# Hybrid decoder layer on one Trainium2 core: the conv gate, the h * c product and the taps stay in the products' PSUM banks

## The chip, the cores and the metric

The kernel runs on one NeuronCore of a Trainium2 chip, as one launch. The metric is the device time in microseconds (us) of that core. TensorE (PE) has the matmuls, VectorE (DVE), ScalarE (ACT) and GpSimd (POOL) the elementwise work, SyncE (SP) issues the transfers. DVE and ACT read and write SBUF and the eight PSUM banks into which PE writes; POOL's operations in this kernel touch SBUF alone.

## The reference, cut to what matters

1024 tokens of width 1024 in float32. The part around the change is the mixer:

```
z = rms_norm(x, norm1_g) @ w_in
cb, cc, ch = split(z[..., :1536], 3)          # B, C, h of the conv group, 512 columns each
rq, rk, rv, rg = split(z[..., 1536:], 4)      # retention: 4 heads of 128 columns each
y_conv = cb * causal_dwconv3(cc * ch, conv_w) # up[t] * w0 + up[t + 1] * w1 + up[t + 2] * w2
y_conv = group_rms_norm(y_conv, conv_norm_g, 8)
o = chunkwise_retention(rotary(q), rotary(k) / sqrt(128), v)
y_ret = group_rms_norm(o, ret_norm_g, 4) * silu(rg)
x = x + concat(y_conv, y_ret) @ w_out
x = x + relu(rms_norm(x) @ w_up) ** 2 @ w_down
out = rms_norm(x)
```

## The kernel before, in words

Tiles are 128 x 1024: 128 columns of a product on the partitions, the 1024 tokens along the free dimension, in two halves of 512 (one PSUM bank each). A float32 matmul is done as three in fp32r: the high and the low part (names `uh`, `ul`, `wh`, `wl`) as high*high, low*high and high*low. The low part of each weight tile is a subtraction, `wl<-r,wh`, on DVE or POOL, behind an ACT cast `wh<-r`.

The first norm's factor per token is R (square root of the mean square, inverted); R2 is R squared and shares its name `ssq` in the rows. It isn't applied to the input but to the projection's result: to B and the gates by R, to C * h by R2.

The columns of `w_in` are 24 tiles f. Tiles 0 to 11 are the conv group in triples i = 0 to 3: C is f = 3i, h is f = 3i + 1, B is f = 3i + 2. Tiles 12 to 19 are q and k, 20 to 23 the gates. The order is the list `IN_TURNS` (line 40): first q and k, then tiles 0, 1, 2, 3, 20 as *whole* tiles (two halves in two banks), then the pairs (4,5), (6,7), (8,9), (10,11), then 21 whole, and 22 and 23 at the end (line 925). A pair is done by one step of a Strassen-Winograd scheme: seven products of half size, `product(n)`, and DVE additions that put them together into the quadrants c11, c12 (first tile of the pair) and acc, c22 (second tile). Its inputs t1 to t4 are made by `rights(j)`: subtractions `xs<-xs` and splits `U<-xs` (ACT cast, then `U<-xs,U` on POOL or DVE).

What happens to a finished half is in `conv_h` (line 677), `conv_b` (702) and `gate` (721), picked by `use` (736) and called from `whole` (744), `pair_in` (824) and the loop at 925. Before the change:

- C: two ACT copies into SBUF (whole tiles), or DVE additions that end in SBUF (pairs).
- h: `a = C * h`, `a *= R2` (POOL or DVE), `cv = a * w2` on ACT, then two DVE taps `cv += a shifted by 1 or 2 * w`.
- B: `o = B * R`, `o *= cv`, then the group norm: a PE product with `blkr` for the mean of squares, and two DVE operations on `o`.
- gates: `g = z * R`, SiLU on ACT, times the retention's output.

A planner decides at build time. Each of these is a Python generator that yields the engines that it could run on (`yield (pool, dve)`) or what it waits for; `background` (428) gives it the engine whose modelled clock is earliest, and writes it into that engine's instruction stream. So a changed operation also moves others. PE's order is fixed by the lists; two pools, `pm` and `pr`, hold four banks each and are taken in turn. A bank can be written again only when its last reader is done.

The retention runs beside tiles 0, 1 and the first `rights`. Its steps are one chain through four engines: PE scores (L625, `b<-v,h`), DVE `h<-b,bk,causal` and `S<-S,b`, ACT `h<-b,bz`, the small DVE and ACT operations on `m` (128x2, the group norm of the step), ACT `h<-b,m`, and PE transposes (L663, `b<-ident,h`).

Of the kernel before, what the change touches and what calls it, by code (L numbers as in the profile page):

```python
# [10 lines left out]
F32 = mybir.dt.float32  # L11
F32R = mybir.dt.float32r
AF = mybir.ActivationFunctionType
ALU = mybir.AluOpType
PSUM = bass.MemoryType.PSUM

P = 128
D = 1024
T = 1024
H = 512  # L20
# [21 lines left out]
SLOT, LOOK, PE_MARGIN, LATE = 2.72, 3.2, 1.2, 0.0  # L42
# [37 lines left out]
def hybrid_layer(  # L80
# [18 lines left out]
    now, clock, procs, got = [0.0], {}, [], {}  # L99
    act = Engine(nc.scalar, 0.13, 0.95, now, clock)  # L100
    pool = Engine(nc.gpsimd, 0.2, 2.5, now, clock)
    dve = Engine(nc.vector, 0.13, 1.04, now, clock, pool)
# [11 lines left out]
    xp = mixer.enter_context(tc.tile_pool(name="xp", bufs=1))  # L114
# [5 lines left out]
    def nm(s):  # L120
        n_[0] += 1
        return f"{s}{n_[0]}"

    def unit(dt=F32, s="u"):
        return big.tile([P, T], dt, tag="u", name=nm(s))
# [6 lines left out]
    def bank(pool_=None):  # L132
        return (pool_ or pm).tile([P, H], F32, tag="b", name=nm("b"))
# [4 lines left out]
    hs = [slice(0, H), slice(H, T)]  # L138
# [90 lines left out]
    for turn in IN_TURNS + IN_END:  # L229
        if isinstance(turn, tuple):  # L230
            o = Left(mix, 1)
# [11 lines left out]
    b = bank(pr)  # L243
# [14 lines left out]
    less_g = cp.tile([P, 4], F32, name="less_g")  # L258
# [26 lines left out]
    R = xp.tile([P, T], F32, name="R")  # L285
# [136 lines left out]
    def spawn(gen, ready=None, late=0.0):  # L422
        Task(gen, now[0] if ready is None else ready, late).go()

    def mark(key, eng):
        got[key] = clock[eng]
# [33 lines left out]
    def slot():  # L460
        now[0] += SLOT
# [58 lines left out]
    def tile_in(evac):  # L520

        out = [bank() for _ in hs]
        for quarter in range(4):
            c, at = quarter // 2, quarter % 2
            if at == 0:
                piece = parts.pop(0)
            mm(
                piece, out,
                lambda n, k: (uh[4 * c + k][:, hs[n]], ul[4 * c + k][:, hs[n]]),
                quarter == 0, quarter == 3, range(2 * at, 2 * at + 2),  # L530
            )
            slot()
            if at:
                prepare()
            if quarter == 1 and once:
                once.pop()()
            if quarter == 3:
                evac(out)
            tick()
# [132 lines left out]
                mark(("retention", p), act)  # L672


    a_of, cvs = {}, {}

    def conv_h(i, half, z, psum):

        a, sl = a_of[i], hs[half]
        eng = dve if psum else (yield (pool, dve))  # L680
        eng.tensor_mul(a[:, sl], a[:, sl], z)
        eng = yield (pool, dve)
        eng.tensor_mul(a[:, sl], a[:, sl], R2[:, sl])
        mark(("a", i, half), eng)
        if half:
            yield "a", i, 0
        yield (act,)
        if i not in cvs:
            cvs[i] = unit(s="cv")
        cv = cvs[i]  # L690
        w = [sm[:, CW + 3 * i + j : CW + 3 * i + j + 1] for j in range(3)]
        act.activation(cv[:, sl], a[:, sl], AF.Copy, scale=w[2])
        yield (dve,)
        for j in (1, 2):
            to = slice(max(sl.start, j), sl.stop)
            dve.scalar_tensor_tensor(
                cv[:, to], a[:, to.start - j : to.stop - j], w[2 - j], cv[:, to],
                ALU.mult, ALU.add,
            )
        mark(("cv", i, half), dve)  # L700

    def conv_b(i, half, z, out, psum):
        sl = hs[half]
        o = out[:, sl]
        eng = dve if psum else (yield (pool, dve))
        eng.tensor_mul(o, z, R[:, sl])
        yield "cv", i, half
        eng = yield (pool, dve)
        eng.tensor_mul(o, o, cvs[i][:, sl])
        y[i] = out  # L710

        def done(rt, less):
            yield (dve,)
            dve.scalar_tensor_tensor(o, o, less_g[:, i : i + 1], rt, ALU.mult, ALU.mult)
            yield (dve,)
            dve.scalar_tensor_tensor(o, less, 1.5, o, ALU.subtract, ALU.mult)
            mark(("y", i, half), dve)

        asked.append((o, blkr, 1.0 / 64, done, clock[eng], LATE * half))

    def gate(h, half, z, g, psum):
        sl = hs[half]
        eng = dve if psum else (yield (pool, dve))
        eng.tensor_mul(g[:, sl], z, R[:, sl])
        yield (act,)
        act.activation(g[:, sl], g[:, sl], AF.Silu)
        yield "o", h, half
        yield (dve,)
        o = o_n[h, half]
        dve.scalar_tensor_tensor(  # L730
            o[:, sl], g[:, sl], sm[:, RG + h : RG + h + 1], o[:, sl], ALU.mult, ALU.mult
        )
        y[4 + h] = o
        mark(("y", 4 + h, half), dve)

    def use(f, half, out, z, psum):

        if f >= 20:
            return gate(f - 20, half, z, out, psum)
        if f % 3 == 1:  # L740
            return conv_h(f // 3, half, z, psum)
        return conv_b(f // 3, half, z, out, psum)

    def whole(f):
        def evac(z):
            if f < 20 and f % 3 == 0:
                out = a_of[f // 3] = unit(s="a")
                for half, sl in enumerate(hs):
                    act.copy(out[:, sl], z[half])
                return  # L750
            out = None if f < 20 and f % 3 == 1 else unit(s="z")
            for half in range(2):
                spawn(use(f, half, out, z[half], True), clock[dve])

        tile_in(evac)

# [61 lines left out]
    for j in range(4):  # L818
        for c, name in ((0, "11"), (1, "21"), (2, "22")):
            k = j + (4 if c else 0)  # L820
            sl = hs[c == 2]
            U.setdefault(name, [None] * 4)[j] = (uh[k][:, sl], ul[k][:, sl])

    def pair_in(fs):
        out = [unit(s="z") for _ in range(2)]
        (c11, c12), (acc, c22) = ([o[:, sl] for sl in hs] for o in out)
        for at, n in enumerate(UP_ORDER):
            if not got.get("pairs") and n in (5, 6, 7, 4):
                for j in range(4):
                    force(({5: "t1", 6: "t2", 7: "t3", 4: "t4"}[n], j))  # L830
            b = product(n, (pm, pr)[at % 2])
            slot()
            prepare()
            ready = None
            if n == 1:
                act.copy(acc, b)
            if n == 2:
                dve.tensor_add(c11, acc, b)
                ready = 0, 0
            if n == 5:  # L840
                b5 = b
            if n in (6, 7, 4):
                dve.tensor_add(acc, acc, b)
            if n == 6:
                dve.tensor_add(c12, acc, b5)
            if n == 7:
                dve.tensor_add(c22, acc, b5)
                ready = 1, 1
            if n == 3:
                dve.tensor_add(c12, c12, b)  # L850
                ready = 0, 1
            if n == 4:
                ready = 1, 0
            if ready:
                f, half, o = fs[ready[0]], ready[1], out[ready[0]]
                if f < 20 and f % 3 == 0:
                    a_of[f // 3] = o
                else:
                    spawn(use(f, half, o, o[:, hs[half]], False), clock[dve], LATE * half)
            tick()  # L860
        got["pairs"] = now[0]

# [48 lines left out]
    for half in range(2):  # L911
        for f, (z, banks, pieces) in ends.items():
            for c in range(2):
                if half == 0:
                    pieces.append(parts.pop(0))
                mm(
                    pieces[c], [banks[half]],
                    lambda n, k: (uh[4 * c + k][:, hs[half]], ul[4 * c + k][:, hs[half]]),
                    c == 0, c == 1,
                )  # L920
                slot()
                if half:
                    prepare()
                if c:
                    spawn(use(f, half, z, banks[half], True), clock[dve])
                tick()
    for half in range(2):
        while any(("split" if half == 0 else "y", idx, half) not in got for idx in range(KT)):
# [322 lines left out]
    for at, (n, p) in enumerate((n, p) for n in MLP_ORDER for p in range(EARLY)):  # L1251
        b = early[p].product(n)
# [106 lines left out]
    def finish(wide, sl, out):  # L1359
        n = sl.stop - sl.start  # L1360
        r = spread(wide)
        if n == H:
            act.copy(R3, r)
            r = R3

        def scale(g):
            o3 = out[g][:, : 2 * n].rearrange("p (a b) -> p a b", b=n)
            dve.tensor_mul(o3, o3, r[:, None, :].to_broadcast([P, 2, n]))
            dst = outT[2 * g * P : 2 * (g + 1) * P, sl].rearrange("(a p) b -> p a b", p=P)
            nc.sync.dma_start(dst, o3)  # L1370

        finishing.extend(lambda g=g: scale(g) for g in range(KT // 2))
# [27 lines left out]
    for sl in (slice(0, H), slice(H, TE)):  # L1400
        n = sl.stop - sl.start
        out = []
# [56 lines left out]
    o = unit(s="end")  # L1459
# [104 lines left out]
```

## Time and profile before

| | us |
|---|---|
| median of three runs | 1071.01 (1069.68 to 1071.92) |
| the profiled execution | 1070.03 |
| its span, first to last instruction | 1068.1 |
| PE busy | 1054.8 (99%) |
| DVE busy | 870.8 (82%) |
| POOL busy | 561.6 (53%) |
| ACT busy | 463.6 (43%) |

The span lies 1.9 us under the profiled execution's own time, and that execution 1.0 us under the median. The granted TensorE clock is full throughout (0.999 on average). PE is busy in 99% of the span, so the table alone says only that time is lost or won where PE waits; the engines' shares do not say where. In a row of the timeline the first number is the start, the second the duration, and `[0.66 <-ACT h L74]` is the idle time of the engine before it and what ended it. Line 74 is the helper that records every elementwise operation, so tiles and operations tell them apart, not lines.

### The profile page before, as it was taken

Reading aid. Unit: us, or ns where it says so; the run is one execution under the profiler, and the core shown is the slowest. Engines: PE = TensorE matmul, PEld = TensorE weight load, DVE = VectorE, ACT = ScalarE, POOL = GpSimd, SP = SyncE. Lnnn points to the kernel's source line nnn. Section 1 sums busy time; section 2 is a strip of 40 time slices with the busy share of each in tenths; the row PEclk is TensorE's granted clock in tenths of the full one; section 3 lists DMA queues with packets and bytes.
Section 4 is the critical chain, followed back from the end, with each engine's and each line's share of the span. In section 5 each row is a group of like instructions: output and inputs, shape, how many; then the busy total and the mean of one; then the engine's idle time right before and its main releaser. Section 6 shows DMA issues by size and latency. Waiting matters only on the chain.

```text
span 1068.1 us, 13853 instructions
## 1 busy us (share of the span) xinstructions
PE 1054.8 (99%) x4860; PEld 879.2 (82%) x4860; DVE 870.8 (82%) x1231; ACT 463.6 (43%) x906; POOL 561.6 (53%) x381
## 2 busy tenths in 40 slices
PE   9999999999999999999999999999999999999997
PEld 8888888788888888788788888888888888888886
DVE  7446546799998665799999989999899899899955
ACT  8211445673437444443343433343443434334453
POOL 6334324367854233559458267277186295384552
PEclk9999999999999999999999999999999999999999
DMA  7121122122223733051221211211301201200204
GB/s 276 65 58 42 38 80 70 63 95 80 69 69 129 256 115 123 11 187 39 61 59 49 79 31 50 90 30 50 99 21 50 89 21 49 90 21 19 69 30 158
DMA packets 39685, 82.25 MB, mean 77 GB/s; under 512 B 4544, under 2 KB 5696, under 8 KB 39616
## 3 DMA queue, kind: packets, MB, share of 16 engines
q1 hardware_dynamic: 39328, 80.85, 23.5%
q8 instruction: 38, 0.62, 0.2%
q10 hardware_dynamic: 288, 0.52, 0.1%
q14 instruction: 31, 0.25, 0.1%
HBM read 71.92 MB, written 9.44 MB: 76 GB/s over the span
## 4 chain that ended last, share of the span: by engine, by line
PE 90%; DVE 6%; ACT 2%; issue 1%; POOL 1%; DVEq 0%; ACTq 0%; POOLq 0%
PE b L403 55%; PE b L1277 23%; PE b L357 4%; PE b L1386 4%; DVE t L74 1%; DVE wl L74 1%; DVE x L74 1%; DVE m L74 1%; ACT h L74 1%; DVE q L74 1%; DVE V L74 1%; PE b L339 0%; PE b L595 0%; PE b L1436 0%; PE b L246 0%
## 5 line engine op out<-in xcount | busy, mean ns | idle before, releaser
L74 ACT CAST wh<-r 128x512 fp32r<-128x512 f32 x286 | 176.6, 620 | 326.4 <-PE b L403 134.4
L403 PE MATMUL b<-U,wh 128*128 128x512 f32 x1024 | 315.8, 390 | 2.0 <-DVE x L74 1.2
L74 DVE TENSOR_TENSOR wl<-r,wh 128x512 fp32r<-128x512 f32 x250 | 232.8, 933 | 89.0 <-ACT wh L74 87.8
L74 POOL TENSOR_TENSOR r<-r,r 128x512 f32<-128x512 f32 x136 | 210.2, 1548 | 114.1 <-DVE wl L74 66.1
L1277 PE MATMUL b<-V,wh 128*128 128x512 f32 x784 | 242.0, 389 | 0.7 <-POOL V L74 0.4
L403 PEld LDWEIGHTS b<-U,wh 128*128 128x128 f32 x1024 | 191.7, 188 | 43.2 <-issue 2.4
L74 DVE TENSOR_TENSOR x<-x,b 128x512 f32<-128x512 f32 (+1 forms) x312 | 195.5, 673 | 28.8 <-PE b L1386 14.3
L403 PE MATMUL b<-U,wl 128*128 128x512 f32 x512 | 199.2, 389 | 0.0
L1277 PEld LDWEIGHTS b<-V,wh 128*128 128x128 f32 x784 | 147.1, 188 | 32.4 <-POOL V L74 0.9
L74 POOL TENSOR_TENSOR t<-t,t 128x512 f32<-128x512 f32 x70 | 106.3, 1523 | 96.4 <-ACT t L74 50.4
L1277 PE MATMUL b<-V,wl 128*128 128x512 f32 x392 | 152.5, 389 | 0.0
L74 POOL TENSOR_TENSOR wl<-r,wh 128x512 fp32r<-128x512 f32 x36 | 51.4, 1432 | 119.3 <-ACT wh L74 116.5
L403 PEld LDWEIGHTS b<-U,wl 128*128 128x128 f32 x512 | 96.1, 188 | 19.9
L403 PE MATMUL b<-uh,wh 128*128 128x512 f32 x304 | 102.3, 396 | 0.0
L403 PE MATMUL b<-ul,wh 128*128 128x512 f32 x304 | 100.5, 390 | 0.0
L403 PE MATMUL b<-uh,wl 128*128 128x512 f32 x304 | 100.2, 389 | 0.0
L1277 PEld LDWEIGHTS b<-V,wl 128*128 128x128 f32 x392 | 73.6, 188 | 15.2
L74 POOL TENSOR_TENSOR V<-t,V 128x512 fp32r<-128x512 f32 x35 | 49.6, 1418 | 67.0 <-ACT V L74 67.0
L74 DVE TENSOR_TENSOR t<-t,b 128x512 f32<-128x512 f32 x112 | 75.8, 677 | 1.7 <-POOL t L74 1.2
L74 ACT ACTIVATE t<-t 128x512 f32<-128x512 f32 x64 | 40.2, 631 | 81.2 <-DVE t L74 80.5
L74 DVE TENSOR_TENSOR V<-t,V 128x512 fp32r<-128x512 f32 x63 | 70.3, 1116 | 0.0
L403 PEld LDWEIGHTS b<-uh,wl 128*128 128x128 f32 x304 | 57.0, 188 | 12.3
(177 smaller groups left out, 1431.3 us busy)
## 6 DMA issues: line engine op xcount, KB each, us to landing
r<-w_up_t SPq DMA_DIRECT2D x64, 256.0 KB, 2.6
r<-w_down_t SPq DMA_DIRECT2D x56, 256.0 KB, 2.7
r<-w_in_t SPq DMA_DIRECT2D x48, 256.0 KB, 2.7
xt<-xT SPq DMA_DIRECT2D x16, 256.0 KB, 5.4
xs<-xT SPq DMA_DIRECT2D x8, 512.0 KB, 5.0
r<-w_out_t SPq DMA_DIRECT2D x16, 256.0 KB, 2.7
x<-xT SPq DMA_DIRECT2D x8, 512.0 KB, 7.9
k<-x SPq DMA_DIRECT2D x6, 512.0 KB, 3.0
```

The costliest lines, as they stand in the source:

```text
L74: return f(out, *args, **kw)
L357: nc.tensor.matmul(vb[i], a[k][:, i * P : (i + 1) * P], b[k // 2][:, vs], start=(k == 0 and a is uh and b is vh), stop=(k == KT - 1 and a ...
L403: nc.tensor.matmul(b, a[:, k, :], rhs(n, k)[r], start=(start and i == 0), stop=(stop and i == len(ops) - 1),)
L1277: nc.tensor.matmul(b, a, r, start=(i == 0), stop=(i == len(ops) - 1))
L1386: nc.tensor.matmul(z, a, b, start=(k == 0 and t == 0), stop=(k == 3 and t == 2))
```

## The change

C is multiplied by R2 as soon as it is in SBUF (`conv_c`), in place of `a * R2` after the product with h. `h * C` is written back into h's bank, ACT and both taps read it there; the last two columns of the first half are copied to a small tile, `edge`, from which the second half's first columns are made with two small taps. In a pair the last addition of a quadrant goes into the bank of a product (`to`) in place of SBUF, and gate and B are multiplied from the bank by R on DVE, never on POOL. The norm's two operations on `o` become one on `less` in its bank (all `b<-b,r`) and one on `o`.

```diff
-    def conv_h(i, half, z, psum):
+    def conv_c(i, half):
+        eng = yield (pool, dve)
         a, sl = a_of[i], hs[half]
-        eng = dve if psum else (yield (pool, dve))
-        eng.tensor_mul(a[:, sl], a[:, sl], z)
-        eng = yield (pool, dve)
         eng.tensor_mul(a[:, sl], a[:, sl], R2[:, sl])
-        mark(("a", i, half), eng)
+        mark(("c", i, half), eng)
+
+    def conv_h(i, half, z):
+        sl = hs[half]
+        yield "c", i, half
+        yield (dve,)
+        dve.tensor_mul(z, z, a_of[i][:, sl])
         if half:
             yield "a", i, 0
         yield (act,)
...
-        act.activation(cv[:, sl], a[:, sl], AF.Copy, scale=w[2])
+        act.activation(cv[:, sl], z, AF.Copy, scale=w[2])
+        if not half:
+            edges[i] = xp.tile([P, 2], F32, tag="edge", name=nm("edge"), bufs=4)
+            act.copy(edges[i], z[:, H - 2 :])
+            mark(("a", i, 0), act)
         yield (dve,)
         for j in (1, 2):
-            to = slice(max(sl.start, j), sl.stop)
+            to = slice(sl.start + j, sl.stop)
             dve.scalar_tensor_tensor(
-                cv[:, to], a[:, to.start - j : to.stop - j], w[2 - j], cv[:, to],
-                ALU.mult, ALU.add,
+                cv[:, to], z[:, : H - j], w[2 - j], cv[:, to], ALU.mult, ALU.add
             )
+            if half:
+                to = slice(sl.start, sl.start + j)
+                dve.scalar_tensor_tensor(
+                    cv[:, to], edges[i][:, 2 - j :], w[2 - j], cv[:, to], ALU.mult, ALU.add
+                )
...
-    def conv_b(i, half, z, out, psum):
+    def conv_b(i, half, z, out):
...
-        eng = dve if psum else (yield (pool, dve))
-        eng.tensor_mul(o, z, R[:, sl])
+        dve.tensor_mul(o, z, R[:, sl])
...
             yield (dve,)
-            dve.scalar_tensor_tensor(o, o, less_g[:, i : i + 1], rt, ALU.mult, ALU.mult)
+            dve.scalar_tensor_tensor(less, less, 1.5, rt, ALU.subtract, ALU.mult)
             yield (dve,)
-            dve.scalar_tensor_tensor(o, less, 1.5, o, ALU.subtract, ALU.mult)
+            dve.scalar_tensor_tensor(o, less, less_g[:, i : i + 1], o, ALU.mult, ALU.mult)
...
-        eng = dve if psum else (yield (pool, dve))
-        eng.tensor_mul(g[:, sl], z, R[:, sl])
+        dve.tensor_mul(g[:, sl], z, R[:, sl])
...
     def whole(f):
...
+                    spawn(use(f, half, out, None), clock[act], 4.0)
...
     def pair_in(fs):
...
+        def finish(i, half, c, a, b, to):
+            f = fs[i]
+            if kind(f) == "c":
+                to = c
+                a_of[f // 3] = out[i]
+            dve.tensor_add(to, a, b)
+            spawn(use(f, half, out[i], to), clock[dve], LATE * half)
...
             if n == 2:
-                dve.tensor_add(c11, acc, b)
-                ready = 0, 0
+                finish(0, 0, c11, acc, b, b)
...
             if n == 7:
-                dve.tensor_add(c22, acc, b5)
-                ready = 1, 1
+                finish(1, 1, c22, acc, b5, b5)
             if n == 3:
-                dve.tensor_add(c12, c12, b)
-                ready = 0, 1
+                finish(0, 1, c12, c12, b, b)
             if n == 4:
-                ready = 1, 0
+                finish(1, 0, acc, acc, b, b)
```

On POOL, between tiles 0 and 2. Before; `a_1532` is C * h of the first triple, `xs_1465`, `xs_1686` and `xs_1687` belong to `rights`, `U_1569` and `U_1912` are its splits:

```order
L74 TENSOR_TENSOR xs_1465<-xs_1465 128x512
L74 TENSOR_TENSOR U_1569<-xs_1465,U_1569 128x512
L74 TENSOR_TENSOR wl_1642<-r_1412,wh_1641 128x512
L74 TENSOR_TENSOR wl_1756<-r_1480,wh_1755 128x512
L74 TENSOR_TENSOR a_1532<-a_1532,ssq 128x512
L74 TENSOR_TENSOR xs_1686<-xs_1686 128x512
L74 TENSOR_TENSOR wl_1875<-r_1526,wh_1874 128x512
L74 TENSOR_TENSOR xs_1687<-xs_1687 128x512
L74 TENSOR_TENSOR U_1912<-xs_1686,U_1912 128x512
```

After; here `z_1532` is C of the first triple, and `xs_1688` what `xs_1686` was:

```order
L74 TENSOR_TENSOR xs_1465<-xs_1465 128x512
L74 TENSOR_TENSOR z_1532<-z_1532,ssq 128x512
L74 TENSOR_TENSOR U_1569<-xs_1465,U_1569 128x512
L74 TENSOR_TENSOR wl_1644<-r_1412,wh_1643 128x512
L74 TENSOR_TENSOR wl_1758<-r_1480,wh_1757 128x512
L74 TENSOR_TENSOR xs_1688<-xs_1688 128x512
L74 TENSOR_TENSOR wl_1877<-r_1526,wh_1876 128x512
L74 TENSOR_TENSOR xs_1689<-xs_1689 128x512
L74 TENSOR_TENSOR wl_1981<-r_1641,wh_1980 128x512
```

The multiplication by R2 stands right behind `xs_1465` and ahead of `U_1569`, three POOL operations earlier, and the split `U_1912` has left POOL.

On DVE at the same place of the program, one retention step, after:

```order
L74 SCALAR_TENSOR_TENSOR m_1554<-m_1554,bq 128x2
L74 TENSOR_TENSOR m_1558<-m_1558 128x2
L74 SCALAR_TENSOR_TENSOR m_1558<-m_1558,m_1554 128x2
L74 SCALAR_TENSOR_TENSOR m_1558<-m_1558 128x2
L74 TENSOR_TENSOR U_1566<-xs_1464,U_1566 128x512
L74 TENSOR_TENSOR z_1532<-z_1532,ssq 128x512
L74 SCALAR_TENSOR_TENSOR h_1592<-b_1587,bk,causal 128x128 x2
L74 SCALAR_TENSOR_TENSOR S_1605<-S_1551,b_1598 128x128 x2
```

Before, the row `z_1532<-z_1532,ssq` isn't there, and the scores' `h` follows `U_1566` directly: the second half of the multiplication by R2 has come in front of the retention's `h` and `S`.

On DVE at the end of the last pair, after; `b_2828` is the bank of the product n = 3, `z_2546` is C, `cv_2772` the convolution, `edge_2774` the two columns:

```order
L74 TENSOR_TENSOR z_2728<-z_2728,b_2807 128x512
L74 TENSOR_TENSOR z_2727<-z_2728,b_2778 128x512
L74 TENSOR_TENSOR wl_2844<-r_2746,wh_2843 128x512
L74 TENSOR_TENSOR b_2828<-z_2727,b_2828 128x512
L74 TENSOR_TENSOR b_2828<-b_2828,z_2546 128x512
L74 SCALAR_TENSOR_TENSOR cv_2772<-b_2828,sm,cv_2772 128x511
L74 SCALAR_TENSOR_TENSOR cv_2772<-edge_2774,sm,cv_2772 128x1
L74 SCALAR_TENSOR_TENSOR cv_2772<-b_2828,sm,cv_2772 128x510
L74 SCALAR_TENSOR_TENSOR cv_2772<-edge_2774,sm,cv_2772 128x2
```

Before, the bank of this product (there `b_2803`) was read once, by the addition:

```order
L74 TENSOR_TENSOR z_2702<-z_2702,b_2782 128x512
L74 TENSOR_TENSOR z_2701<-z_2702,b_2758 128x512
L74 TENSOR_TENSOR z_2701<-z_2701,b_2803 128x512
L74 TENSOR_TENSOR z_2536<-z_2536,z_2701 128x512
```

Now five operations use it, with one of ACT between the product with C and the first tap. The second half of tile 21 is the next to write that bank.

## Rows read from the trace of the kernel before

**Rows 1.** PE waits by line: releaser, total us, count, longest

```profile
PE b L663 <- ACT h L74: 2.3, 5, 0.7
```

**Rows 2.** Windows, us: busy time and count of PE, PEld, DVE, ACT, POOL; clock

```profile
213.00:345.00 132.00, 132.00 (x584) 109.28 (x584) 120.22 (x133) 71.91 (x115) 90.01 (x60) 1.00 0.27 87
```

**Rows 3.** PE timeline, retention: start, duration, instruction, idle before

```profile
179.86 0.39 PE L625 MATMUL b<-v,h 128*128 128x128 f32 x2
181.20 0.38 PE L663 MATMUL b<-ident,h 128*128 128x128 f32 x2
...
197.00 0.44 PE L663 MATMUL b<-ident,h 128*128 128x128 f32 x2 [0.66 <-ACT h L74]
...
206.61 0.59 PE L663 MATMUL b<-ident,h 128*128 128x128 f32 x2 [0.73 <-ACT h L74]
...
210.32 0.58 PE L663 MATMUL b<-ident,h 128*128 128x128 f32 x2 [0.35 <-ACT h L74]
```

**Rows 4.** POOL timeline, 172 to 208 us

```profile
172.28 1.29 POOL L74 TENSOR_TENSOR xs<-xs 128x512 f32<-128x512 f32 x1 [0.63 <-DVE xs L74]
176.75 1.30 POOL L74 TENSOR_TENSOR U<-xs,U 128x512 fp32r<-128x512 f32 x1 [3.17 <-ACT U L74]
...
193.57 1.27 POOL L74 TENSOR_TENSOR a<-a,ssq 128x512 f32<-128x512 f32 x1
194.81 1.26 POOL L74 TENSOR_TENSOR xs<-xs 128x512 f32<-128x512 f32 x1
...
207.73 1.30 POOL L74 TENSOR_TENSOR U<-xs,U 128x512 fp32r<-128x512 f32 x1 [1.99 <-ACT U L74]
```

**Rows 5.** DVE timeline, the same stretch

```profile
174.00 0.16 DVE L74 SCALAR_TENSOR_TENSOR m<-m,bq 128x2 f32<-128x2 f32 x1 [0.94 <-ACT h L74]
...
176.18 0.69 DVE L74 TENSOR_TENSOR U<-xs,U 128x512 fp32r<-128x512 f32 x1 [1.20 <-ACT U L74]
176.79 0.60 DVE L74 SCALAR_TENSOR_TENSOR h<-b,bk,causal 128x128 f32<-128x128 f32 x2
...
193.90 0.97 DVE L74 TENSOR_TENSOR m<-m 128x2 f32<-128x2 f32 x1 [0.27 <-ACT m L74]
...
194.90 1.19 DVE L74 SCALAR_TENSOR_TENSOR m<-m,m 128x2 f32<-128x2 f32 x1
...
208.21 0.83 DVE L74 SCALAR_TENSOR_TENSOR m<-m,bq 128x2 f32<-128x2 f32 x1 [0.61 <-ACT h L74]
```

**Rows 6.** POOL timeline, 222 to 225 us

```profile
222.94 1.39 POOL L74 TENSOR_TENSOR wl<-r,wh 128x512 fp32r<-128x512 f32 x1 [2.84 <-ACT wh L74]
```

**Rows 7.** DVE timeline, 222 to 225 us

```profile
222.50 0.69 DVE L74 TENSOR_TENSOR U<-xs,U 128x512 fp32r<-128x512 f32 x1
...
223.10 1.79 DVE L74 TENSOR_TENSOR U<-xs,U 128x512 fp32r<-128x512 f32 x1
```

**Rows 8.** ACT timeline of the step at 175 us

```profile
175.53 1.14 ACT L74 CAST U<-xs 128x512 fp32r<-128x512 f32 x2
177.49 0.62 ACT L74 ACTIVATE h<-b,bz 128x128 f32<-128x128 f32 x2 [0.82 <-DVE h L74]
...
179.68 0.62 ACT L74 ACTIVATE h<-b,m 128x128 f32<-128x128 f32 x2 [0.62 <-DVE m L74]
```

**Rows 9.** Groups by operation, 160 to 345 us: busy, mean ns | idle before

```profile
L74 DVE TENSOR_TENSOR z<-z,b 128x512 f32<-128x512 f32 x28 | 19.0, 679 | 0.4
L74 DVE SCALAR_TENSOR_TENSOR cv<-z,sm,cv 128x512 f32<-128x512 f32 x4 | 5.8, 1461 | 0.1
L74 ACT ACTIVATE cv<-z,sm 128x512 f32<-128x512 f32 x4 | 2.9, 725 | 11.1 <-POOL z L74 11.1
```

**Rows 10.** PE timeline at the end of the last pair

```profile
305.76 0.39 PE L484 MATMUL b<-s,blkr 128*128 128x512 f32 x1
...
311.43 0.62 PE L403 MATMUL b<-uh,wh 128*128 128x512 f32 x2
```

**Rows 11.** DVE timeline there

```profile
309.07 2.19 DVE L74 TENSOR_TENSOR z<-z,b 128x512 f32<-128x512 f32 x3
```

More of the change, by code (lines that the diff above doesn't have):

```diff
@@ L672, in retention @@
                 mark(("retention", p), act)
-    a_of, cvs = {}, {}
-    def conv_h(i, half, z, psum):
+    a_of, cvs, edges = {}, {}, {}
+    def conv_c(i, half):
+        eng = yield (pool, dve)
         a, sl = a_of[i], hs[half]
-        eng = dve if psum else (yield (pool, dve))
-        eng.tensor_mul(a[:, sl], a[:, sl], z)
-        eng = yield (pool, dve)
         eng.tensor_mul(a[:, sl], a[:, sl], R2[:, sl])
-        mark(("a", i, half), eng)
+        mark(("c", i, half), eng)
[4 more added lines that the diff above has]
+        dve.tensor_mul(z, z, a_of[i][:, sl])
         if half:
@@ L713, in done, with gate @@
             yield (dve,)
-            dve.scalar_tensor_tensor(o, o, less_g[:, i : i + 1], rt, ALU.mult, ALU.mult)
+            dve.scalar_tensor_tensor(less, less, 1.5, rt, ALU.subtract, ALU.mult)
             yield (dve,)
-            dve.scalar_tensor_tensor(o, less, 1.5, o, ALU.subtract, ALU.mult)
+            dve.scalar_tensor_tensor(o, less, less_g[:, i : i + 1], o, ALU.mult, ALU.mult)
             mark(("y", i, half), dve)
         asked.append((o, blkr, 1.0 / 64, done, clock[eng], LATE * half))
-    def gate(h, half, z, g, psum):
+    def gate(h, half, z, g):
         sl = hs[half]
-        eng = dve if psum else (yield (pool, dve))
-        eng.tensor_mul(g[:, sl], z, R[:, sl])
+        dve.tensor_mul(g[:, sl], z, R[:, sl])
         yield (act,)
@@ L734, in gate, with kind, use @@
         mark(("y", 4 + h, half), dve)
[L736 to L742, printed above, removed]
+    def kind(f):
+        return "g" if f >= 20 else "chb"[f % 3]
+    def use(f, half, out, z):
+        if kind(f) == "g":
+            return gate(f - 20, half, z, out)
+        if kind(f) == "c":
+            return conv_c(f // 3, half)
+        if kind(f) == "h":
+            return conv_h(f // 3, half, z)
+        return conv_b(f // 3, half, z, out)
     def whole(f):
         def evac(z):
-            if f < 20 and f % 3 == 0:
-                out = a_of[f // 3] = unit(s="a")
+            out = None if kind(f) == "h" else unit(s="z")
+            if kind(f) == "c":
+                a_of[f // 3] = out
                 for half, sl in enumerate(hs):
                     act.copy(out[:, sl], z[half])
+                    spawn(use(f, half, out, None), clock[act], 4.0)
                 return
-            out = None if f < 20 and f % 3 == 1 else unit(s="z")
             for half in range(2):
-                spawn(use(f, half, out, z[half], True), clock[dve])
+                spawn(use(f, half, out, z[half]), clock[dve])
         tile_in(evac)
@@ L826, in pair_in @@
         (c11, c12), (acc, c22) = ([o[:, sl] for sl in hs] for o in out)
+        def finish(i, half, c, a, b, to):
+            f = fs[i]
+            if kind(f) == "c":
+                to = c
+                a_of[f // 3] = out[i]
+            dve.tensor_add(to, a, b)
+            spawn(use(f, half, out[i], to), clock[dve], LATE * half)
         for at, n in enumerate(UP_ORDER):
@@ L833, in pair_in @@
             prepare()
-            ready = None
             if n == 1:
@@ L837, in pair_in @@
             if n == 2:
-                dve.tensor_add(c11, acc, b)
-                ready = 0, 0
+                finish(0, 0, c11, acc, b, b)
             if n == 5:
                 b5 = b
-            if n in (6, 7, 4):
+            if n in (6, 7):
                 dve.tensor_add(acc, acc, b)
@@ L846, in pair_in @@
             if n == 7:
-                dve.tensor_add(c22, acc, b5)
-                ready = 1, 1
+                finish(1, 1, c22, acc, b5, b5)
             if n == 3:
-                dve.tensor_add(c12, c12, b)
-                ready = 0, 1
+                finish(0, 1, c12, c12, b, b)
             if n == 4:
-                ready = 1, 0
[L854 to L859, printed above, removed]
+                finish(1, 0, acc, acc, b, b)
             tick()
@@ L924, in hybrid_layer @@
                 if c:
-                    spawn(use(f, half, z, banks[half], True), clock[dve])
+                    spawn(use(f, half, z, banks[half]), clock[dve])
                 tick()
```

## The prediction, made before the changed kernel ran

> **What bounds the kernel now.** I read the table of engine shares first: PE is busy in 99% of the span, so an edit on DVE, POOL or ACT counts only where PE waits for them. The list of PE's waits says where that is. The part that the change touches, from the first tiles to the end of the projection, has one entry of weight: L663, the retention's transposes, which wait for ACT's `h`, 2.3 us in five waits [rows 1]. Next, the windows: from 213 to 345 us, where all four pairs, tiles 2, 3, 20 and 21 are evacuated, PE is busy for 132.00 of 132.00 us, while DVE is busy for 120.22 and POOL for 90.01 [rows 2]. A shorter DVE buys nothing there. It can only lose: if a bank is held so long that PE finds it taken.
>
> The retention's steps come third. Three of the five waits lie in the stretch that changes, at 197.00, 206.61 and 210.32 (0.66, 0.73 and 0.35 us) [rows 3]. Their origin is on the engine behind ACT. DVE's `m` operations on two columns take 0.16 us where nothing is beside them, but the one at 193.90 took 0.97 and ended with POOL's `a<-a,ssq`, the one at 194.90 took 1.19 and ended with POOL's `xs<-xs`, and the one at 208.21 took 0.83 and ended with POOL's split U [rows 4, 5]. So an SBUF operation of DVE that starts beside one of POOL ends with it. Where DVE has the next one queued, POOL still goes first: `wl` starts at 222.94, when DVE's U from 222.50 is nearly done; the next U of DVE starts at 223.10 and takes 1.79, to 0.56 us behind the end of `wl` at 224.33 [rows 6, 7]. An operation that reads a bank isn't held: the scores' `h` from 176.79 (two of 128x128, with a factor and a mask in SBUF) takes 0.60 us beside POOL's U from 176.75 [rows 4, 5], and 28 additions of a bank average 679 ns, where taps in SBUF average 1461 [rows 9].
>
> [...]
>
> **The change, part by part.**
>
> *Bank operations in place of SBUF ones.* Taps, products and the norm's factor move into banks, at about 0.68 us in place of up to 1.46 [rows 9]. In 213 to 345 us this is worth 0 on the path, since PE never waits [rows 2]; the cover is the queue of matmuls. [...]
>
> *The multiplication of C by R2 moves into a retention step.* This is the term that costs. (a) Before, POOL's `xs` ends at 172.28 + 1.29 = 173.57. Now the multiplication of the first half follows at once, for 1.27 us as `a<-a,ssq` took, until 174.83. DVE's `m` at 174.00 would start in it and end with it: 174.83 in place of 174.16, +0.67 on the chain. (b) ACT's two casts U [rows 8] start that much later, DVE's U runs to 177.53 in place of 176.87. POOL's U, whose cast is ready, then takes its turn and ends 1.14 us later (as 224.33 follows DVE's 223.19), at 178.67; the queued second half of the multiplication ends 0.56 us behind it, at 179.23. (c) Only then comes the scores' `h`, at 179.15 (it began 0.08 before its forerunner's end) in place of 176.79: the chain is +2.36. Behind it on DVE stand `S` and the step's `m`, and ACT's `h` and then PE wait for those. (d) PE: the score product at 179.86 writes a bank that ACT's `h<-b,bz` has to have read; that ends at 177.49 + 0.62 + 2.36 = 180.47, so PE waits 0.6 there. L663 at 181.20 needs ACT's `h<-b,m`, which ends at 179.68 + 0.62 + 2.36 = 182.66, or 1.46 late; together +1.5 us.
>
> From below: if DVE's second multiplication went ahead of POOL's U it would take 0.69, the chain would be +1.35 at `h`, and L663's operand would be ready at 181.65, 0.45 late. If nothing collided, 0. From above: both collisions in full, 2 x 1.3 + 0.69 = 3.3 on the chain, +2.4 for PE after the 0.9 that it has in hand (181.20 less 180.30). I take 1.5, since 222 to 225 us show this very order.
>
> *One collision less at 197.* `a<-a,ssq` is gone from 193.57. At most the 0.97 us become 0.16. But `xs` stands right behind it in POOL's stream, its input was ready, and so it moves up into the same place. From both sides 0 and 0.81; I take 0.2, near the lower end, and the shift falls from +1.5 to +1.3. The wait at 206.61 hangs on work that the change leaves there: 0.
>
> *One split less on POOL at 207.73.* U moves to DVE, ahead of the `m` operations. The `m` at 208.21 falls from 0.83 to 0.16, a gain of 0.67 on the chain, of which PE can use its wait of 0.35 and the slower transposes behind it (0.58 in place of 0.38 or 0.44), 0.55. Shift +0.75. From both sides 0 (U on DVE itself delays `m`) and 0.67.
>
> *Banks of tile 1 held by the taps.* Before, one multiplication freed each bank; now ACT's scaling and two taps, the last ones behind the retention's `m` operations. Tile 2 writes these banks next, just behind 210.32. At 0.68 us a tap the last one ends about when PE arrives: I take +0.2, between 0 and 2 x 0.78 = 1.56 (each tap at 1461 ns). Shift +0.95.
>
> *The bank of product n = 3 of the last pair.* Before, it was free with the last of three additions, 309.07 + 2.19 = 311.26; tile 21's second half needs it at 311.66 (the second of two matmuls from 311.43) [rows 10, 11], 0.4 us in hand, and the additions stood behind two taps of 3.2 us. Now: the product ends behind the two norm matmuls at 306.15, then the addition into the bank, the multiplication by C and one `wl` ahead of them (3 x 0.68), ACT's scaling 0.73 [rows 9], two hand-overs of 0.25, a tap 0.68, an edge tap of at most 0.2 (as a small operation alone), the second tap 0.68: 310.98. In hand 0.68, cost 0.
>
> *The rest.* The edge copy and six edge taps are small operations, some 0.2 us each and at worst 1.19 [rows 5]; in 213 to 345 us they lie beside full PE. The norm's DVE operations stay two, one of them in a bank: 0. SP's transfers and PE's list are the same but for a few places of the norm's products.
>
> Sum: +1.5 - 0.2 - 0.55 + 0.2 = +0.95. The profiled execution takes 1070.03 and would take 1070.98; it lies 0.98 under the median of its runs, 1071.01, so the forecast in the median's terms is 1071.96, told as 1071.9. About 0.2%, 2.1 us, is what a measurement of this kernel can tell from no change.
>
> **The rivals.**
>
> *B, little is lost.* The second multiplication goes ahead of POOL's split, or the retention makes good what it lost before 197. Then 0.45 - 0.2 - 0.55 + 0.2 = -0.1: 1070.9. For it: the later waits take up delay. Against: rows 6 and 7.
>
> *B2, the collisions all vanish.* If operations on banks leave the retention's DVE work free, the 2.3 us of rows 1 are the most that can go: 1068.7. Against: two of the five waits lie ahead of the change, and 206.61 isn't touched.
>
> *C, slower: a bank is held.* If an operation in a bank, reading and writing it or with SBUF operands beside POOL, takes as long as the tap in SBUF, 1.46, the last pair's chain has four of them: 4 x 0.78 = 3.1, less 0.68 in hand, 2.45 us that PE waits at 311.66; at tile 2's banks up to 1.56. With 0.95: +5.0, 1076. It decides from 0.68 + 0.68/4 = 0.85 us for each such operation. For it: rows 9 have no tap from a bank with an SBUF accumulator. Against: `h<-b,bk,causal` has such operands and wasn't held.
>
> That the change does not do what it says: the order shows that it does, so this gets no chance of its own.
>
> **How the numbers follow.** Forecast 0.64 (its own range 1070.9 to 1073.0), B 0.14, B2 0.05, C 0.17. The range leaves out the lower part of B2 and the upper half of C: 1069.7 to 1074.2. Faster by over 0.2% is under 1068.9, most of B2 and a little of B: 0.07. Slower by over 0.2% is over 1073.15: C and the upper tail of the forecast, 0.19. Within it: 0.74.
>
> **What would show it.** Right: DVE's `m` near 174.0 lasts about 0.8 us; `z<-z,ssq` on DVE near 177 takes 1.7; L663 waits near 181 for the first time; taps from a bank take about 0.68; PE stays full from tile 2 to 345. Wrong: no wait at 181 (B); PE waits at a whole tile's first matmul for DVE's `cv` (C); more DVE time in bank operations than 0.85 us each; or a wait of PE for `wl` or `wh` in the pairs, which I have at nothing.

## The result, and the profile after

The changed kernel takes 1074.0 us (median of 10 runs, 1073.03 to 1074.6) against 1071.63 us for the kernel before (10 runs). The ratio is 1.0021 with a 95% interval of 1.0013 to 1.0029: slower by 2.25 us (1.4 to 3.1). The forecast was +0.95 us, with a range of 1069.7 to 1074.2. The sign and the mechanism of its largest term came out; another term, which stood at nothing, is 1.4 us.

The page of the profile, busy time by engine, after:

```profile
span 1072.0 us, 13870 instructions
PE 1056.4 (99%) x4860; PEld 880.0 (82%) x4860; DVE 863.8 (81%) x1244; ACT 464.1 (43%) x910; POOL 549.0 (51%) x376
```

DVE has 7.0 us less to do (870.8 before) and POOL 12.6 less (561.6), and the kernel is slower all the same. The list of PE's waits of after, which answers to [rows 1], says why:

```profile
PE b L663 <- ACT h L74: 2.3, 5, 0.7
PE b L403 <- DVE cv L74: 1.4, 2, 1.2
...
PE b L403 <- DVE t L74: 0.7, 1, 0.7
...
PE b L625 <- ACT h L74: 0.4, 1, 0.4
```

The transposes' total is the same 2.3 us, but not in the same places. The entries for `cv`, `L625` (the retention's scores) and `t` are new. PE's timeline of after, against [rows 3] and [rows 10]:

```profile
180.97 0.49 PE L625 MATMUL b<-v,h 128*128 128x128 f32 x2 [0.43 <-ACT h L74]
183.17 0.44 PE L663 MATMUL b<-ident,h 128*128 128x128 f32 x2 [0.59 <-ACT h L74]
...
198.80 0.44 PE L663 MATMUL b<-ident,h 128*128 128x128 f32 x2 [0.34 <-ACT h L74]
...
208.41 0.59 PE L663 MATMUL b<-ident,h 128*128 128x128 f32 x2 [0.74 <-ACT h L74]
...
211.59 0.53 PE L663 MATMUL b<-ident,h 128*128 128x128 f32 x2
...
212.58 0.50 PE L403 MATMUL b<-uh,wh 128*128 128x512 f32 x1 [0.22 <-DVE cv L74]
...
314.76 0.47 PE L403 MATMUL b<-uh,wh 128*128 128x512 f32 x1 [1.15 <-DVE cv L74]
...
501.30 0.70 PE L403 MATMUL b<-U,wh 128*128 128x512 f32 x2 [0.70 <-DVE t L74]
```

PE runs the same 4860 matmuls in both kernels, in the same order but for the places of some products of the norm between 266 and 329 us. So the start of one instruction after, less its start before, is how late PE is there. This execution was already 0.42 us late before the first of these waits (at 113 us, and at 10 us too), which is taken off:

| PE at (us of before) | later by | less 0.42 | forecast |
|---|---|---|---|
| 181.20, L663 | 1.97 | 1.55 | 1.5 |
| 197.00, L663 | 1.80 | 1.38 | 1.3 |
| 206.61, L663 | 1.80 | 1.38 | 1.3 |
| 210.32, L663 | 1.27 | 0.85 | 0.75 |
| tile 2 under way, 211.21 | 1.70 | 1.28 | 0.95 |
| tile 21 under way, 311.88 | 3.19 | 2.77 | 0.95 |
| behind 498 | 3.92 | 3.50 | 0.95 |

Up to 210.32 the forecast's steps come out within 0.1 us. Tile 1's bank adds 0.43 in place of 0.2. Then 1.4 us come at the bank of the last pair (1.80 late at 311.20, 3.19 at 311.88), and in this execution another 0.65 near 500.

The origin of the first term, DVE of after, against [rows 5], and POOL of after, against [rows 4]:

```profile
174.41 0.83 DVE L74 SCALAR_TENSOR_TENSOR m<-m,bq 128x2 f32<-128x2 f32 x1 [0.94 <-ACT h L74]
...
177.27 0.69 DVE L74 TENSOR_TENSOR U<-xs,U 128x512 fp32r<-128x512 f32 x1 [1.20 <-ACT U L74]
177.88 1.80 DVE L74 TENSOR_TENSOR z<-z,ssq 128x512 f32<-128x512 f32 x1
179.60 0.60 DVE L74 SCALAR_TENSOR_TENSOR h<-b,bk,causal 128x128 f32<-128x128 f32 x2
```

```profile
173.95 1.28 POOL L74 TENSOR_TENSOR z<-z,ssq 128x512 f32<-128x512 f32 x1
177.83 1.30 POOL L74 TENSOR_TENSOR U<-xs,U 128x512 fp32r<-128x512 f32 x1 [2.60 <-ACT U L74]
```

The two-column `m` lasts 0.83 us and ends with POOL's multiplication (175.23). DVE's own multiplication by R2 waits for POOL's split (to 179.13) and ends 0.55 us behind it, at 179.68. The scores' `h` starts 2.39 us later than before, the start's 0.42 taken off (179.60 less 176.79 less 0.42); forecast 2.36.

The origin of the large term, DVE and POOL at the last pair, after:

```profile
308.00 1.40 DVE L74 TENSOR_TENSOR z<-z,b 128x512 f32<-128x512 f32 x2
309.32 0.69 DVE L74 TENSOR_TENSOR wl<-r,wh 128x512 fp32r<-128x512 f32 x1
309.93 0.69 DVE L74 TENSOR_TENSOR b<-z,b 128x512 f32<-128x512 f32 x1
310.65 0.70 DVE L74 TENSOR_TENSOR b<-b,z 128x512 f32<-128x512 f32 x1
312.11 0.75 DVE L74 SCALAR_TENSOR_TENSOR cv<-b,sm,cv 128x511 f32<-128x511 f32 x1 [0.76 <-ACT cv L74]
312.77 1.18 DVE L74 SCALAR_TENSOR_TENSOR cv<-edge,sm,cv 128x1 f32<-128x1 f32 x1
313.88 0.73 DVE L74 SCALAR_TENSOR_TENSOR cv<-b,sm,cv 128x510 f32<-128x510 f32 x1
314.54 0.20 DVE L74 SCALAR_TENSOR_TENSOR cv<-edge,sm,cv 128x2 f32<-128x2 f32 x1
```

```profile
312.66 1.29 POOL L74 TENSOR_TENSOR wl<-r,wh 128x512 fp32r<-128x512 f32 x1 [4.94 <-ACT wh L74]
```

Read the fifth to the seventh row of DVE with POOL's row: the tap on one column lasts 1.18 us and ends with POOL's `wl` at 313.95. The large tap behind it, which has the bank, ends at 314.61, and PE starts at 314.76. The same small tap beside nothing lasts 0.21 (at 211.66).

### The profile page after: what moved, and what is told of

Same layout as the page of the kernel before. It is cut to its first block, busy times and chain, and to the rows that moved or that the text cites. A ratio compares the mean times of both kernels' runs of the same rounds, so it can differ in the third digit from the quotient of the medians.

```text
span 1072.0 us, 13870 instructions
## 1 busy us (share of the span) xinstructions
PE 1056.4 (99%) x4860; PEld 880.0 (82%) x4860; DVE 863.8 (81%) x1244; ACT 464.1 (43%) x910; POOL 549.0 (51%) x376
## 4 chain that ended last, share of the span: by engine, by line
PE 85%; DVE 8%; ACT 3%; POOL 2%; issue 2%; DMA 1%; DVEq 0%; SPq 0%; ACTq 0%; POOLq 0%
PE b L403 52%; PE b L1295 22%; PE b L357 4%; PE b L1404 4%; ACT h L74 1%; DVE wl L74 1%; DVE t L74 1%; DVE m L74 1%; DVE x L74 1%; POOL r L74 1%; POOL x L74 1%; DMA r<-w_down_t 1%; DVE q L74 1%; DVE V L74 1%; PE b L246 0%
## 5 line engine op out<-in xcount | busy, mean ns | idle before, releaser
L74 DVE TENSOR_TENSOR wl<-r,wh 128x512 fp32r<-128x512 f32 x242 | 221.2, 916 | 93.7 <-ACT wh L74 92.9
L74 POOL TENSOR_TENSOR wl<-r,wh 128x512 fp32r<-128x512 f32 x44 | 60.2, 1370 | 138.4 <-ACT wh L74 137.4
```

Of the source, the lines that this page charges most:

```text
L74: return f(out, *args, **kw)
```

## The experiments

Ratios are to the kernel before on the same chip, with 95% intervals. The timing separates about 0.9 us; what is smaller is read from PE's waits. A second profile of each of the two kernels (e8 and e9, below) gives these waits again within 0.02 us.

**e1: the two small taps last.** Nothing but this order differs from the changed kernel.

```diff
         for j in (1, 2):
             to = slice(sl.start + j, sl.stop)
             dve.scalar_tensor_tensor(
                 cv[:, to], z[:, : H - j], w[2 - j], cv[:, to], ALU.mult, ALU.add
             )
+        for j in (1, 2):
             if half:
                 to = slice(sl.start, sl.start + j)
```

> Only the order of four taps of DVE changes: both large taps from the bank first, then the two small ones on the edge columns. Nothing else moves on any engine. Theory (three mechanisms: C * R2 in a retention step +1.4 us, tile 1's bank +0.5, and the one-column edge tap that stands between the two large taps and ends only with POOL's wl, which holds the last pair's bank: +1.3): PE's wait at 314.8 falls from 1.15 us to 0.2 or less, the one at 212.6 from 0.22 to about 0.1, the waits near 181 and 183 stay; some 1.2 us less than the changed kernel, about 1.0 us above before. Rival (work in a bank is slow in itself, by the taps or the product with C): both large taps still stand in the chain, the wait at 314.8 stays over 0.8 us. Rival (the loss lies at the start or in the output projection, where the profile has 0.4 and 0.65 us more): nothing changes.

Measured: ratio 1.0016 (1.0007 to 1.0025), which the timing does not separate from the changed kernel's 1.0021. So the traces decide. DVE, POOL and PE of e1, at the last pair:

```profile
311.59 1.53 DVE L74 SCALAR_TENSOR_TENSOR cv<-b,sm,cv 128x511 f32<-128x511 f32 x2 [0.76 <-ACT cv L74]
313.04 0.66 DVE L74 SCALAR_TENSOR_TENSOR cv<-edge,sm,cv 128x1 f32<-128x1 f32 x2
```

```profile
312.14 1.29 POOL L74 TENSOR_TENSOR wl<-r,wh 128x512 fp32r<-128x512 f32 x1 [4.95 <-ACT wh L74]
```

```profile
313.27 0.47 PE L403 MATMUL b<-uh,wh 128*128 128x512 f32 x1 [0.29 <-DVE cv L74]
```

Both taps on the bank take 1.53 us together, the second of them wholly beside POOL's `wl`, so work in a bank is not slow. PE's wait falls from 1.15 to 0.29 (0.2 or less was expected). The edge tap is shown as the cause of 0.86 us; 0.3 has another cause. At tile 2 nothing is won (0.22), against the 0.1 that was expected: the two taps there take 1.52 us with the small one between them (211.00 to 212.52 in the changed kernel), and in e3, where it stands behind them, 1.52 too.

**e2: the first triple's C * R2 later.** Both of its multiplications now stand on DVE, in a gap near 190 us.

```diff
-                    spawn(use(f, half, out, None), clock[act], 4.0)
+                    spawn(use(f, half, out, None), clock[act] + (15.0 if f == 0 else 0.0), 4.0)
```

> Only the first triple's multiplication of C by R2 moves: both halves on DVE, ahead of a later retention step's h (near 192), where ACT is busy until 195, in place of POOL at 174 and DVE at 178. Theory: the DVE m operation near 174 is back at 0.16 us, the waits of PE near 181 (0.43) and 183 (0.59) are gone, 1.5 us; 0 to 0.4 of it comes back at the wait near 198.8, which stands on another collision (POOL's xs and wl with m); the wait at 314 stays at about 1.15. Some 1.2 us less than the changed kernel. Rival (retention catches up anyway by 213, so that the move costs nothing at the end): the time stays that of the changed kernel, and PE's start of tile 2 is no earlier than 0.3 us. Rival (start and output projection): no change.

Measured: ratio 1.0002 (0.9993 to 1.0011), some 2 us less than the changed kernel; the intervals do not overlap. PE's timeline of e2 has no wait between 178 and 206 us. The two left up to tile 2, then DVE's multiplications and two of its `m` operations:

```profile
206.86 0.58 PE L663 MATMUL b<-ident,h 128*128 128x128 f32 x2 [0.59 <-ACT h L74]
...
211.03 0.50 PE L403 MATMUL b<-uh,wh 128*128 128x512 f32 x1 [0.22 <-DVE cv L74]
```

```profile
190.90 1.29 DVE L74 TENSOR_TENSOR z<-z,ssq 128x512 f32<-128x512 f32 x2
...
195.18 0.97 DVE L74 TENSOR_TENSOR m<-m 128x2 f32<-128x2 f32 x1 [0.27 <-ACT m L74]
196.18 0.16 DVE L74 SCALAR_TENSOR_TENSOR m<-m,m 128x2 f32<-128x2 f32 x1
```

The same two multiplications take 1.29 us together in this gap, in which POOL too sat idle before (183.09 to 192.32) and after (185.91 to 195.15), where they took 1.28 on POOL and 1.80 on DVE. Not only the waits at 181 and 183 are gone but the one at 197 too, where up to 0.4 us was expected to come back. The two `m` operations there, 0.97 and 1.19 us before [rows 5], take 0.97 and 0.16. The changed kernel has the same two lengths there (0.95 and 0.16), and its POOL has no `a<-a,ssq` there any more: `xs` moves up and ends at 197.69, with the first of the two. The chain is 1.03 us shorter by that. PE, which had waited 0.66 there, is 1.05 us earlier than before at 206.61, the next wait (this execution's start, 1.30 us late, taken off). The changed kernel is 1.38 late there. The rival by which the retention catches up anyway falls.

**e3: both edits.**

> The two edits of the runs before together. Theory: 2.2 to 2.5 us less than the changed kernel, that is within 0.5 us of the kernel before (ratio 0.9995 to 1.0005). If the loss has another part (the norm's factor, the start, the output projection), 0.7 us or more stays above before. Rival that bank work pays off on its own: clearly below before, by over 1 us.

Measured: ratio 0.9990 (0.9981 to 0.9999), 1.1 us below before. No third part of the loss is left over. The waits at the two banks are still there, the second one shorter:

```profile
209.83 0.50 PE L403 MATMUL b<-uh,wh 128*128 128x512 f32 x1 [0.21 <-DVE cv L74]
...
311.19 0.47 PE L403 MATMUL b<-uh,wh 128*128 128x512 f32 x1 [0.30 <-DVE cv L74]
```

What pays for them is the shorter retention of e2: with the start taken off, PE is 1.0 us earlier than before at 206.61, and 0.4 us from 311.88 on. No run has that gain without the operations in banks, so it is not shown that these gain anything by themselves.

**e4: the pairs' quadrants back in SBUF.** Whole tiles as in the changed kernel.

```diff
         def finish(i, half, c, a, b, to):
             f = fs[i]
+            to = c
             if kind(f) == "c":
-                to = c
                 a_of[f // 3] = out[i]
```

> Of the changed kernel, only the pairs' quadrants go back into SBUF (the last addition writes the tile's SBUF half, and gate, product with C and both taps read there); whole tiles keep their banks, and C * R2 stays early. Theory: from tile 2 to 345 us PE stays full as before, although DVE has 5 to 10 us more to do there; the bank wait at 314 is gone: 1.0 to 1.3 us less than the changed kernel, with the waits near 181 and 183 as they are. Rival (DVE's relief in the pairs is worth something on the path): PE waits appear in the pairs and the time is that of the changed kernel or more.

Measured: ratio 1.0024 (1.0015 to 1.0033), no less than the changed kernel's; the expectation, 1.0 to 1.3 us less, missed. The window from 213 to 345 us, first of after, then of e4, and e4's PE row at the bank:

```profile
213.00:345.00 132.00, 130.85 (x577) 107.92 (x576) 113.41 (x144) 72.31 (x119) 77.42 (x55) 1.00 0.26 88
```

```profile
213.00:345.00 132.00, 131.38 (x578) 108.34 (x579) 120.06 (x143) 71.70 (x119) 80.23 (x55) 1.00 0.26 86
```

```profile
314.52 0.50 PE L403 MATMUL b<-uh,wh 128*128 128x512 f32 x1 [0.62 <-DVE z L74]
```

DVE's 6.7 us more leave PE full except at this one place. There the bank waits for a plain addition, which stands behind two slow SBUF taps of 2.95 us from 309.00 on. The kernel before has such taps too (3.21 us) and no wait, but there they start 3.06 us earlier, and PE is only 2.09 us later in e4. PE wins 0.5 us there, not 1.2. So the bank is late from either side: with the quadrants in SBUF by the queue ahead of the addition, with the quadrants in banks by the chain behind it.

**e5 and e6: the bank handed back at the product.** Both stand on e3. The second half's h * C goes into C's SBUF half, and ACT and the large taps read it there: in the last triple (e5, `(3,)`), in the first and the last (e6).

```diff
-        dve.tensor_mul(z, z, a_of[i][:, sl])
+        o = a_of[i][:, sl] if half and i in (0, 3) else z
+        dve.tensor_mul(o, z, a_of[i][:, sl])
+        z = o
```

> On top of the two edits together (e3): for the last pair alone the second half's product with C is written into C's SBUF half, and ACT and the large taps read it there, so that the bank is free behind that product. No instruction moves. Theory (the bank is what PE waits for at 311.2): that wait, 0.30 us with 0.47 lost, is gone, the two large taps take 1.2 to 1.5 us each in place of 0.75 and cost nothing, since PE does not wait for cv; 0.4 to 0.5 us less than e3 in PE's list, too little for the timing. Rival (DVE is the limit there): the slower taps delay the next additions and another wait of PE, for DVE's z or wl, takes its place within the next 10 us.

> As the run before, and the same for the second half of tile 1, whose bank tile 2 waits for near 209.8 (0.22 us waited, 0.58 lost with its successor). Theory: both bank waits are gone, 1.0 us less than e3 in PE's list, and the time about 1.5 us below the kernel before (ratio 0.998 to 0.9995). Rival (the slower taps now stand in front of DVE's split and of tile 2's evacuation): a wait for wl or for a bank appears between 210 and 225 and gives half of it back.

Measured: e5 0.9999 (0.9990 to 1.0009) against e3's 0.9990. The timing does not separate the two, and could not show the 0.4 us that were expected; in e5's trace the wait at 311 is gone. e6 0.9982 (0.9973 to 0.9991), 1069.23 us at the median: 1.9 us below before (1.0 to 2.9), the lowest ratio of all. PE in e6 has one wait left between 178 and 320 us, and is full from 213 to 345:

```profile
205.51 0.59 PE L663 MATMUL b<-ident,h 128*128 128x128 f32 x2 [0.66 <-ACT h L74]
```

```profile
213.00:345.00 132.00, 132.00 (x583) 109.19 (x582) 112.56 (x143) 71.19 (x116) 77.59 (x55) 1.00 0.26 87
```

No other wait took the place of the two up to 345 us, so the taps in SBUF, of which the last pair's two take 2.44 us (from 308.78) for 1.53 from a bank in e1, cost nothing there. With the start taken off, PE is 1.4 us earlier than before behind the last pair, and 0.75 behind a wait of 0.70 near 497. The timed 1.9 is more than that, and no trace shows where the rest lies.

**e7: the norm's factor as before**, on the changed kernel.

```diff
-            dve.scalar_tensor_tensor(less, less, 1.5, rt, ALU.subtract, ALU.mult)
+            dve.scalar_tensor_tensor(o, o, less_g[:, i : i + 1], rt, ALU.mult, ALU.mult)
             yield (dve,)
-            dve.scalar_tensor_tensor(o, less, less_g[:, i : i + 1], o, ALU.mult, ALU.mult)
+            dve.scalar_tensor_tensor(o, less, 1.5, o, ALU.subtract, ALU.mult)
```

> The changed kernel with the group norm's factor as before (two operations on o, none on less in its bank). Theory: the norm's factor has no part in the loss; the waits near 181, 183 and 314 stay within 0.2 us, and the time is that of the changed kernel (1.0013 to 1.0030 of before). DVE has some 4 us more to do between 213 and 345 us. Rival (the norm's operations on a bank hold it and cost PE): 0.5 us or more less than the changed kernel.

Measured: ratio 1.0025 (1.0014 to 1.0036), the time of the changed kernel. The wait at the bank is 1.34 us in place of 1.15, DVE from 213 to 345 has 2.8 us more. The norm's part is not shown to cost anything.

**e8 and e9: both kernels once more**, for the start and the wait near 500 us.

> The kernel before, unchanged, for a second profile. Open point: the changed kernel's profile has 0.4 us more at the start and a wait of PE near 500 us (0.70 for DVE's t in the output projection's successor) that the profile of before has not. If these are chances of one execution, they differ between two profiles of the same kernel, here by up to 1 us before 113 us and by 0 or 0.65 at 497; the waits of the retention (0.66, 0.73, 0.35) and the free banks return within 0.05 us. If the 0.65 belongs to the change, it is absent here.

> The changed kernel, unchanged, for a second profile. The waits near 181 (0.43), 183 (0.59), 213 (0.22) and 315 (1.15) return within 0.05 us, since their causes lie in the order of instructions; the one near 501 (0.70) may be there or not if it is a chance of the execution, and has to be there if it belongs to the change.

Measured: 1071.15 and 1073.76 us, one execution each. PE's waits of e9:

```profile
181.14 0.49 PE L625 MATMUL b<-v,h 128*128 128x128 f32 x2 [0.41 <-ACT h L74]
183.33 0.44 PE L663 MATMUL b<-ident,h 128*128 128x128 f32 x2 [0.59 <-ACT h L74]
...
314.95 0.47 PE L403 MATMUL b<-uh,wh 128*128 128x512 f32 x1 [1.15 <-DVE cv L74]
...
501.24 0.70 PE L403 MATMUL b<-U,wh 128*128 128x512 f32 x2 [0.45 <-DVE t L74]
```

The waits return, those at 181, 183 and 315 above as well as the one near 213 (0.23). The start is a chance of one execution: the same L663 starts at 112.96 us in one profile of before and at 113.74 in the other, and between 112.81 (e1) and 114.25 (e2) in the eleven profiles. The wait at 500 is 0.70 in one profile of after and 0.45 in the other. It is absent from both profiles of before, from e3 and from e7, which has all other delays of the changed kernel, and present in e1, e2 and e4 to e6. So neither PE's lateness nor one of the edits alone decides it. Its cause stays open, and so does whether one kernel has it in one execution and not in another. The timed difference, 2.25 us, is nearer to the 2.85 us without it than to the 3.50 with it.

## Why the prediction was right, and the term that it sized wrongly

That the time lies in the range is in part luck. It is 2.1 us above the forecast of 1071.9 and 0.2 us below the range's end. It is also over 1073.15, to which the prediction gave 0.19. The range reached that far for the forecast's tail and for half of rival C, whose mechanism did not occur. Of the signs of being right, `m` of 0.83, `z<-z,ssq` of 1.80 and the wait near 181 came, and taps of 0.73 to 0.75 us in place of 0.68. But PE did not stay full (130.85 of 132.00 us), and it waits for `cv` in whole tiles (212.58 and 314.76), which stood there as the sign of C.

*C * R2 in the retention step, +1.5.* Right in every part: `m` 0.83 us long, the split ahead of the queued multiplication, `h` 2.39 us late, PE 1.55. e2 takes it away alone and is some 2 us faster than the changed kernel, more than this term, as the shorter retention at 197 then reaches PE. Rival B fell with it.

*One collision less at 197, -0.2.* Measured 1.55 to 1.38, and here the size is luck. DVE of after:

```profile
196.74 0.95 DVE L74 TENSOR_TENSOR m<-m 128x2 f32<-128x2 f32 x1 [0.27 <-ACT m L74]
197.73 0.16 DVE L74 SCALAR_TENSOR_TENSOR m<-m,m 128x2 f32<-128x2 f32 x1
```

`xs` moved up into the place, as argued, and holds the first `m`. But the prediction left out the next one, which `xs` had held for 1.19 us [rows 5] and which now takes 0.16. So the chain wins 1.03 us there, more than the bound of 0.81. The chain had been 2.42 us late (196.15 for 193.31) while PE was 1.55 late. At ACT's `h<-b,m` it is 1.38 late, and PE with it. The 0.17 is the difference of the two, which the sum didn't follow.

*One split less on POOL, -0.55.* Measured 1.38 to 0.85, 0.53. The `m` operation is back at 0.15 us (at 210.10).

*Banks of tile 1, +0.2.* Mis-sized: PE waits 0.22 there, and is 1.28 late behind it in place of 0.85, so 0.43. The two taps take 1.52 us, where the sum had 2 x 0.68. The bank was given back by the last large tap at 212.52, some 0.2 us behind PE. e6 shows the cause by removing it.

*The bank of product n = 3 of the last pair, 0.* This is the step that failed. It had the bank free at 310.98 on before's clock. PE was 1.80 us later there, so 312.78; measured 314.61, a difference of 1.83. Two things were left out. The order has two additions ahead of `wl` (its first two rows in the section on the change), and the sum did not count them: DVE reaches `wl` at 309.32, not at the product's end, 307.95, 1.37 us. And the edge tap stood at 0.2 as an operation alone, although the next paragraph of the prediction had 1.19 as its worst case: it took 1.18, so 0.98. The other steps were shorter by 0.5 together. Of this 0.43 are the two hand-overs around ACT's operation, which stood in the sum at 0.25 each, a figure that no run shows: ACT starts 0.03 us behind the product with C (311.38 for 311.35), the first tap 0.04 behind ACT (312.11 for 312.07). 1.83 less the 0.68 in hand is 1.15, the wait in the trace. In PE's lateness it is 1.4: PE's matmuls start 0.23 us apart ahead of the wait (312.99 and 313.22), 1.54 across it (314.76) and 0.31 behind it (315.07). e1 removes the second cause and leaves 0.29; e5 gives the bank back earlier and leaves none. No run takes the two additions away, so the first cause is read from the rows alone.

*Bank operations, 0 on the path.* Right where PE has work queued: 6.8 us less of DVE from 213 to 345 us (113.41 for 120.22) buy nothing in the changed kernel. Too strong in general: e4 takes that relief away and PE waits 0.62 at a bank, e6 keeps most of it and PE doesn't wait there.

Rival C had the right place and the wrong mechanism. It asked for bank operations of 0.85 us or more. They took 0.69 to 0.75, and the bank was held by what stood between and ahead of them.

## What to carry to other kernels

When work moves into a bank, write down the whole chain from the product's end to the last reader, in the order of the queue: each operation that stands ahead, and each small SBUF operation in between, at the price that it has beside POOL (1.18 us here, 0.21 alone). Put the last reader of a bank ahead of everything that only shares its loop (e1: the wait fell from 1.15 to 0.29 us). And when one operand becomes ready earlier, don't let it be multiplied at once: an operation without urgency belongs in a gap of the chain beside it, not at its own earliest time (e2: some 2 us).

## What the runs showed of the hardware

The price of an SBUF tap is POOL's, not SBUF's. Rows 9 had 1461 ns for it, and the prediction read that as the price of SBUF. In e6 the taps of tile 1 stand twice on DVE, first from a bank, then from SBUF, with POOL idle:

```profile
204.97 1.53 DVE L74 SCALAR_TENSOR_TENSOR cv<-b,sm,cv 128x511 f32<-128x511 f32 x2
...
208.09 1.53 DVE L74 SCALAR_TENSOR_TENSOR cv<-z,sm,cv 128x511 f32<-128x511 f32 x2
```

Two taps take 1.53 us from either. The trace of before had it too, on two SBUF taps of tile 1 with POOL idle:

```profile
206.07 1.53 DVE L74 SCALAR_TENSOR_TENSOR cv<-a,sm,cv 128x511 f32<-128x511 f32 x2
```

These rows show no difference between a bank and SBUF. Beside POOL two SBUF taps took longer: 3.21 us in the trace of before, from 305.94, with POOL's two `wl` from 305.61 to 308.60. What a bank buys is that POOL doesn't hold the operation: the eight taps of 511 columns from banks average 747 ns after, between 160 and 345 us, beside POOL or not (0.74 for the one from 283.45, with POOL's `z<-z,cv` from 283.62 to 284.92), where the four of rows 9 averaged 1461.

The length of an SBUF operation on DVE is no guide to what it costs beside POOL: one column took 1.18 us (0.21 alone), two columns 0.83 (0.16). In both of these POOL's operation starts first (312.66 for 312.77, 173.95 for 174.41), and DVE's ends with it. For a DVE operation that was queued behind another of its own, POOL came in between in both places shown here (it ends at 179.13 and 224.33, and had started 0.05 and 0.16 us before DVE's row), and DVE ended 0.55 us behind it.
